# Side work of a two-layer diffusion step: the waits between its stages are set anew

## Chip, core and metric

One core of one Trainium2 chip runs the whole program in one launch. The metric is the device time of an execution in microseconds, as the median of several.

## What is computed

One inference step of a two-layer network over 384 columns: 128 context tokens and 256 latent tokens, model width 1024. Per layer (from the reference):

```python
h = _rmsnorm(x, norm_mix[d]) * (1.0 + ca) + sa        # sa, ca, ga, sm, cm, gm from silu(c) @ w_mod[d] + b_mod[d]
q, k, v, gb, gc, xin, u, vs = _project(h, w_in[d])
q = _apply_axial_rope(q, rope); k = _apply_axial_rope(k, rope)      # latent tokens only
att = _diff_attention(q, k_all, v_all, lam, subln[d], lam_init)     # softmax(1) - lam * softmax(2), then rmsnorm
conv = gb * _short_conv(gc * xin, conv_w[d], conv_b[d])
cmlp = _chunk_mlp(u, vs, w_s[d], b_s[d])
x = x + ga * (concat([att, conv, cmlp]) @ w_out[d])
h = _rmsnorm(x, norm_mlp[d]) * (1.0 + cm) + sm
x = x + gm * (relu(h @ w_up[d]) ** 2 @ w_down[d])
```

There are four attention heads, each with two 64-dim components of q and k; the context keys and values of the cache come in front of the latent ones. A final rmsnorm ends it; the new context keys and values are outputs too.

## The kernel before

**Products.** Activations lie transposed, features on the partitions, 384 columns wide. Each weight chunk of 128 x 1024 (512 KB, tile `raw`) is loaded by SyncE's DMA queue (L187), cut by ScalarE into a rounded high part (`whi`, L201) and by VectorE into the rest (`wlo`, L203). A product step, `mm3` at L217, is three matmuls: high weights by high activations, high by low, low by high (L220, L221, L222; L449 to L451 where tokens are the rows, `nat`). Activations are split the same way: `hh` and `hl`.

**Order of a layer.** Mixer: keys and queries of the first heads (`pkq`; three heads in layer 0, two in layer 1), values (`nat`, 512 wide), then `pk` and `pq` of the remaining heads and two short convolutions of three products each (`pgc`, `pxi`, `pgb`), then the chunk inputs (`nat`, 256 wide) and `pu`, then the output product `po2`. After it the MLP in two halves (`pup`, `pdn`). In layer 0 TensorE also does the products with `wmod` that give five of the modulation vectors (`pm`, L262, in groups of two loads), and VectorE does the others as long weighted sums (L315, tile `junk`), a pair for each load.

**Side work.** Everything else is side work: the norm and its scaling (`normed`, L370 hh on ScalarE, L373 hl on VectorE), rotary positions (`rope_apply`: a shuffle on VectorE, L656, then three steps on GpSimd, L657 to L659), the split of keys (`keys`: kh casts on ScalarE, L674 and L677, kl on VectorE, L678), of queries (`queries`: L690 and L693), attention, convolution, and the column sums of the shift (`shift_products`: `psh`, its copy `shb` at L468, `psb` at L472). An attention unit is one head by one block of 128 query columns; three units make a head. In it come the scores `sc` (L738 to L742), the negative row maximum `nm` (L746), the exponentials (L751), their scaling (L755 to L759), transposes `pt` (L763), the copy `ats` (L774); the last unit of a head then does `po`, probabilities by values (L786), squares (L792), the rsqrt and its refinement, the scaled `o` (L801), transposes `pot` (L807) and the result into `y` (L810, L812).

**What sets the order.** Nothing is scheduled at run time: TensorE, ScalarE, VectorE and GpSimd carry out their instructions in the order in which the program issues them, and each waits for its inputs. Side work is written as Python generators that yield between two stages. `yield n` says that the next stage is issued n ticks later, and `tick` is called after every product step, where it issues every stage that has come due:

```python
    def tick(n=1):
        for _ in range(n):
            clock[0] += 1
            while queue and queue[0][0] <= clock[0]:
                step()
```

The numbers n stand in the table `WAIT` (L35), one entry for each place, as a pair for layer 0 and layer 1. So a number there sets how many product steps TensorE does between one stage and the next, and with it the place of the stage in the queue of each engine. An instance, the end of an attention unit:

```python
            yield wt["at6"]
            cols = slice(h * P, h * P + P)
            po = acc_tile("po")
```

Here `at6` ticks lie between the issue of the copy `ats` and that of the products `po` that read it. Likewise `k0` lies ahead of the rotation of a key, `k1` between the rotation and the kh casts of L674, `k2` ahead of the casts of L677; `q0`, `q1`, `q2` do this for queries; `fh0` lies ahead of the third head of `first_heads`; `mods` is the number of ticks between two groups of `pm`, `sums0` the delay of the first L315. `mods0` and `sums0` are read in layer 0 only.

Of the kernel before, what the change touches and what calls it, by code (L numbers as in the profile page):

```python
# [31 lines left out]


WAIT = {
    "sums_up": (8, 7),  # L35
    "sums_down": (5, 0),
    "hid0": (1, 1),
    "hid1": (3, 3),
    "later": (4, 4),
    "later2": (4, 6),  # L40
    "spread": (2, 0),
    "final": (4, 3, 3, 3),
    "rstd": (3, 9),
    "at0": (1, 1),
    "at1": (2, 1),
    "at2": (3, 3),
    "at3": (2, 2),
    "at4": (5, 5),
    "at5": (1, 3),
    "at6": (4, 2),  # L50
    "at7": (2, 2),
    "at8": (2, 2),
    "at9": (2, 2),
    "at10": (3, 4),
    "at11": (1, 1),
    "at12": (1, 1),
    "k0": (1, 1),
    "k1": (5, 5),
    "k2": (1, 3),
    "q0": (1, 1),  # L60
    "q1": (5, 6),
    "q2": (1, 2),
    "fh0": (14, 14),
    "fh1": (2, 5),
    "fh2": (2, 2),
    "fh3": (5, 5),
    "cv0": (1, 3),
    "cv1": (2, 2),
    "cv2": (2, 3),
    "cm0": (1, 1),  # L70
    "sy": (2, 2),
    "normed": (3, 3),
    "wait_normed": (1, 12),
    "mix": (4, 4),
    "heads": (4, 1),
    "mods": (9, 0),
    "mods0": (2, 0),
    "sums": (7, 0),
    "sums0": (58, 0),
    "unit0": (24, 24),  # L80
    "head": (24, 24),
    "late": (0, 5),
# [1029 lines left out]
```

## Time and profile before

| | us |
|---|---|
| Median of three executions | 907.21 (906.78 to 910.43) |
| Profiled execution | 906.61 |
| Its span, first to last instruction | 904.8 |
| TensorE busy | 876.9 |
| VectorE busy | 651.6 |
| ScalarE busy | 481.7 |
| GpSimd busy | 84.2 |

The mean granted clock of TensorE is 0.995 of full speed. In the rows below a time is the start in microseconds from the start of the span, then follow the duration, the engine, the line, the operation, the tiles (out<-in), their shape and, in brackets, how long the engine was idle before it and what ended that. A row of waits reads: engine and line that waited, what it waited for, the total in microseconds, how many times, the longest.

### The profile page before, as it was taken

The page shows a single profiled execution, that of the slowest core. Times are in us where ns is not written, and L with a number is a line of the kernel's source. Part 1 is how long each engine was busy: PE and PEld are TensorE (multiplying, and loading weights), DVE is VectorE, ACT ScalarE, POOL GpSimd, SP SyncE. Part 2 cuts the span into 40 slices and gives each one's busy share as a digit, 9 for nine tenths or more (in the row PEclk, how much of TensorE's full clock was granted, in tenths as well). Part 3 has the DMA queues.
Part 4 walks back from the last instruction along what each step waited for, and adds up shares of the span by engine and source line. Part 5 has one row for each costly group of instructions (what it writes and reads, how often), then busy time and mean ns, then how long its engine had stood idle before and what let it go on. Part 6 is the DMA issues. An engine that isn't in the chain of part 4 may idle for free.

```text
span 904.8 us, 14504 instructions
## 1 busy us (share of the span) xinstructions
PE 876.9 (97%) x5476; PEld 841.8 (93%) x5476; DVE 651.6 (72%) x1214; ACT 481.7 (53%) x949; POOL 84.2 (9%) x84
## 2 busy tenths in 40 slices
PE   5999989999999999999998999999999999999996
PEld 4867878999999999999997889999999999999996
DVE  5697887889888777889979877568886334555333
ACT  4568765447662236654336786444675223665331
POOL 1013310030000000000113340002000000000021
PEclk9999999999999999999999999999999999999998
DMA  9977657555667655557663323234565333433302
GB/s 346 330 280 258 231 168 271 167 166 167 205 190 235 230 187 190 197 189 236 213 218 102 131 73 117 92 97 134 175 220 167 123 133 117 133 124 118 116 1 70
DMA packets 48470, 156.55 MB, mean 173 GB/s; under 512 B 5392, under 2 KB 11024, under 8 KB 48400
## 3 DMA queue, kind: packets, MB, share of 16 engines
q1 hardware_dynamic: 48400, 155.63, 51.8%
q8 instruction: 43, 0.70, 0.3%
q14 instruction: 27, 0.22, 0.1%
HBM read 152.98 MB, written 2.62 MB: 172 GB/s over the span
## 4 chain that ended last, share of the span: by engine, by line
PE 84%; DVE 7%; ACT 4%; POOL 2%; issue 1%; DMA 1%; SPq 0%; DVEq 0%; ACTq 0%; POOLq 0%
PE pdn L220 10%; PE pdn L222 10%; PE pdn L221 10%; PE pup L221 10%; PE pup L220 9%; PE pup L222 9%; PE po L220 2%; PE po L221 2%; PE po L222 2%; PE pm L262 2%; PE pkq L220 2%; PE pkq L221 2%; PE pkq L222 1%; DVE wlo L203 1%; POOL rt L658 1%
## 5 line engine op out<-in xcount | busy, mean ns | idle before, releaser
L201 ACT CAST whi<-raw 128x1024 fp32r<-128x1024 f32 x182 | 190.4, 1052 | 286.8 <-PE pdn L221 153.9
L203 DVE TENSOR_TENSOR wlo<-raw,whi 128x1024 fp32r<-128x1024 f32 x182 | 224.6, 1240 | 61.4 <-ACT whi L201 61.2
L220 PE MATMUL pdn<-ah,whi 128*128 128x384 f32 (+2 forms) x528 | 174.7, 331 | 0.0
L221 PE MATMUL pdn<-al,whi 128*128 128x384 f32 (+2 forms) x528 | 174.6, 331 | 0.0
L222 PE MATMUL pdn<-ah,wlo 128*128 128x384 f32 (+2 forms) x528 | 174.6, 331 | 0.0
L220 PE MATMUL pup<-hh,whi 128*128 128x386 f32 x512 | 174.2, 340 | 0.0
L221 PE MATMUL pup<-hl,whi 128*128 128x386 f32 x512 | 173.7, 339 | 0.3
L222 PE MATMUL pup<-hh,wlo 128*128 128x386 f32 x512 | 172.8, 338 | 0.0
L315 DVE SCALAR_TENSOR_TENSOR junk<-raw,cb 128x1024 bf16<-128x1024 f32 x112 | 136.7, 1220 | 0.4
L221 PEld LDWEIGHTS pdn<-al,whi 128*128 128x128 f32 x528 | 99.2, 188 | 0.0
L220 PEld LDWEIGHTS pdn<-ah,whi 128*128 128x128 f32 x528 | 99.2, 188 | 0.0
L222 PEld LDWEIGHTS pdn<-ah,wlo 128*128 128x128 f32 x528 | 99.2, 188 | 0.0
L221 PEld LDWEIGHTS pup<-hl,whi 128*128 128x128 f32 x512 | 96.9, 189 | 1.1 <-DVE hl L388 0.9
L220 PEld LDWEIGHTS pup<-hh,whi 128*128 128x128 f32 x512 | 96.4, 188 | 0.3
L222 PEld LDWEIGHTS pup<-hh,wlo 128*128 128x128 f32 x512 | 96.5, 188 | 0.0
L337 POOL TENSOR_TENSOR sacc<-sacc,sq 128x384 f32<-128x384 f32 x23 | 29.6, 1285 | 667.5 <-ACT sq L330 533.6
L927 ACT ACTIVATE relu<-relu,ub 128x128 f32<-128x128 f32 (+1 forms) x128 | 51.3, 449 | 17.4 <-DVE relu L924 17.4
L399 DVE SCALAR_TENSOR_TENSOR x<-pdn,modv,x 128x128 f32<-128x128 f32 (+1 forms) x62 | 23.0, 413 | 43.9 <-PE pdn L222 43.9
L931 DVE TENSOR_TENSOR al<-relu,ah 128x384 fp32r<-128x384 f32 x64 | 35.6, 556 | 15.2 <-ACT ah L929 14.9
L220 PE MATMUL po<-y,whi 128*128 128x384 f32 x128 | 43.0, 336 | 0.0
L222 PE MATMUL po<-y,wlo 128*128 128x384 f32 x128 | 42.8, 334 | 0.0
L221 PE MATMUL po<-y,whi 128*128 128x384 f32 x128 | 42.8, 334 | 0.0
(202 smaller groups left out, 1413.7 us busy)
## 6 DMA issues: line engine op xcount, KB each, us to landing
raw<-in_wall_dram SPq DMA_DIRECT2D x182, 512.0 KB, 3.6
raw<-in_wmodT_dram SPq DMA_DIRECT2D x56, 512.0 KB, 4.3
raw<-in_wmod_dram SPq DMA_DIRECT2D x40, 512.0 KB, 5.7
raws<-in_wall_dram SPq DMA_DIRECT2D x6, 512.0 KB, 7.1
x<-in_xT_dram SPq DMA_DIRECT2D x8, 192.0 KB, 8.0
out_dram<-x SPq DMA_DIRECT2D x4, 256.0 KB, 2.6
mix<-in_cv_dram SPq DMA_DIRECT2D x2, 256.0 KB, 5.0
mix<-in_ws_dram SPq DMA_DIRECT2D x2, 256.0 KB, 5.2
```

The source lines that it names most:

```text
L201: nc.scalar.copy(hi, r)
L203: nc.vector.tensor_sub(lo, r, hi.bitcast(F32))
L220: mm(out, wh[wsl], ah[asl], start=first, stop=False)
L221: mm(out, wh[wsl], al[asl], start=False, stop=False)
L222: mm(out, wl[wsl], ah[asl], start=False, stop=last)
L262: mm(pm[32 * j : 32 * j + 32, own], sct[:, kt, :], w[:, (4 * k + j) * width : (4 * k + j + 1) * width], start=(kt == 0), stop=(kt == KT - 1),)
L315: nc.vector.scalar_tensor_tensor(junk, w, 1.0, cb[:, g], ALU.mult, ALU.mult, accum_out=mr[:, dt, g : g + 1])
L337: eng.tensor_add(stat["acc"], stat["acc"], sq)
L399: nc.vector.scalar_tensor_tensor(x[:, dt, a:b], pacc[:, a:b], gate[:, dt, g : g + 1], x[:, dt, a:b], ALU.mult, ALU.add)
L658: nc.gpsimd.tensor_mul(s, s, rp[:, 1])
L927: nc.scalar.activation(r[:, s0:s1], r[:, s0:s1], AF.Relu, bias=ub[:, g : g + 1])
L931: nc.vector.tensor_sub(al[:, i], r, ah[:, i].bitcast(F32))
```

## The change

Only numbers of `WAIT` change. The same instructions are issued, and the sum of work of each engine is the same. The core of the diff, the entries of which the text speaks:

```diff
-    "at6": (4, 2),
+    "at6": (2, 2),
-    "k0": (1, 1),
-    "k1": (5, 5),
+    "k0": (1, 3),
+    "k1": (9, 6),
-    "q2": (1, 2),
-    "fh0": (14, 14),
+    "q2": (2, 4),
+    "fh0": (8, 14),
-    "mods": (9, 0),
+    "mods": (7, 0),
-    "sums0": (58, 0),
+    "sums0": (61, 1),
...
```

Changed as well: `sums_up` (8, 7) to (8, 8), `hid0` (1, 1) to (1, 3), `hid1` (3, 3) to (3, 4), `spread` (2, 0) to (1, 0), `rstd` (3, 9) to (3, 10), `at7` (2, 2) to (3, 3), `at8` (2, 2) to (2, 3), `at11` (1, 1) to (2, 1), `at12` (1, 1) to (2, 3), `cv0` (1, 3) to (1, 5), `sy` (2, 2) to (4, 1), `wait_normed` (1, 12) to (2, 12), `mods0` (2, 0) to (2, 1).

The order of instructions differs in the first two thirds of layer 0's mixer and the start of its `po2`, in layer 1's mixer, and on VectorE and ScalarE in the first half of layer 1's MLP. GpSimd's order is the same throughout.

ScalarE, layer 0, ahead of the copy shb that the shift product psb reads. kh are the key casts, qs the query casts, e the exponentials; - stands before, + now:

```order
-L201 CAST whi<-raw 128x1024
+L677 CAST kh<-mix 64x384 x2
+L201 CAST whi<-raw 128x1024
+L751 ACTIVATE e,s<-sc,nm 128x128 x2
 L674 CAST kh<-mix 64x384 x2
-L677 CAST kh<-mix 64x384 x2
-L751 ACTIVATE e,s<-sc,nm 128x128 x2
 L690 CAST qs<-mix 64x256 x2
 L757 ACTIVATE e<-e,s 128x128
 L468 COPY shb<-psh 128x256
+L677 CAST kh<-mix 64x384 x2
```

The second casts of one head have moved behind shb, and those of the head before it have moved up to this place from further ahead.

ScalarE, layer 0, at the products pk and pq of the fourth head. L725 and L726 copy the new queries, L774 is the copy ats:

```order
-L674 CAST kh<-mix 64x384 x2
-L757 ACTIVATE e<-e,s 128x384
-L774 COPY ats<-pt 128x3x128
-L677 CAST kh<-mix 64x384 x2
+L757 ACTIVATE e<-e,s 128x384
+L774 COPY ats<-pt 128x3x128
 L201 CAST whi<-raw 128x1024
 L725 ACTIVATE qp_106<-pq 64x128 x2
 L726 ACTIVATE mix<-pq 128x256
+L674 CAST kh<-mix 64x384 x2
 L751 ACTIVATE e,s<-sc,nm 128x128 x2
+L677 CAST kh<-mix 64x384 x2
```

Both pairs of kh casts, ahead of the query copies before, stand behind them now.

VectorE, layer 1, during the values product, before. t and hl are the norm's tiles, kl_104 the low part of a key, rt the rotation's:

```order
L656 STREAM_SHUFFLE rt<-mix 128x256
L678 TENSOR_TENSOR kl_104<-mix,kh 64x384 x2
L203 TENSOR_TENSOR wlo<-raw,whi 128x1024
L362 SCALAR_TENSOR_TENSOR t<-x,amix_94,rstd 128x128
L362 SCALAR_TENSOR_TENSOR t<-x,amix_94,rstd 128x256
L373 SCALAR_TENSOR_TENSOR hl<-t,modv_92,hh 128x128
L373 SCALAR_TENSOR_TENSOR hl<-t,modv_92,hh 128x256
```

The same place now:

```order
L656 STREAM_SHUFFLE rt<-mix 128x256
L203 TENSOR_TENSOR wlo<-raw,whi 128x1024
L362 SCALAR_TENSOR_TENSOR t<-x,amix_94,rstd 128x128
L362 SCALAR_TENSOR_TENSOR t<-x,amix_94,rstd 128x256
L373 SCALAR_TENSOR_TENSOR hl<-t,modv_92,hh 128x128
L373 SCALAR_TENSOR_TENSOR hl<-t,modv_92,hh 128x256
L678 TENSOR_TENSOR kl_104<-mix,kh 64x384 x2
```

The two subtractions kl_104 stand behind this pair of hl.

More of the change, by code (lines that the diff above doesn't have):

```diff
@@ L34 @@
 WAIT = {
-    "sums_up": (8, 7),
+    "sums_up": (8, 8),
     "sums_down": (5, 0),
-    "hid0": (1, 1),
-    "hid1": (3, 3),
+    "hid0": (1, 3),
+    "hid1": (3, 4),
     "later": (4, 4),
     "later2": (4, 6),
-    "spread": (2, 0),
+    "spread": (1, 0),
     "final": (4, 3, 3, 3),
-    "rstd": (3, 9),
+    "rstd": (3, 10),
     "at0": (1, 1),
@@ L49 @@
     "at5": (1, 3),
-    "at6": (4, 2),
-    "at7": (2, 2),
-    "at8": (2, 2),
+    "at6": (2, 2),
+    "at7": (3, 3),
+    "at8": (2, 3),
     "at9": (2, 2),
     "at10": (3, 4),
-    "at11": (1, 1),
-    "at12": (1, 1),
-    "k0": (1, 1),
-    "k1": (5, 5),
+    "at11": (2, 1),
+    "at12": (2, 3),
+    "k0": (1, 3),
+    "k1": (9, 6),
     "k2": (1, 3),
@@ L66 @@
     "fh3": (5, 5),
-    "cv0": (1, 3),
+    "cv0": (1, 5),
     "cv1": (2, 2),
@@ L70 @@
     "cm0": (1, 1),
-    "sy": (2, 2),
+    "sy": (4, 1),
     "normed": (3, 3),
-    "wait_normed": (1, 12),
+    "wait_normed": (2, 12),
     "mix": (4, 4),
     "heads": (4, 1),
-    "mods": (9, 0),
-    "mods0": (2, 0),
+    "mods": (7, 0),
+    "mods0": (2, 1),
     "sums": (7, 0),
-    "sums0": (58, 0),
+    "sums0": (61, 1),
     "unit0": (24, 24),
```

## The prediction

> **What bounds the kernel now.** I read the page first: busy times, the row of granted clock, the chain that ended last.
>
> ```profile
> PE 876.9 (97%) x5476; PEld 841.8 (93%) x5476; DVE 651.6 (72%) x1214; ACT 481.7 (53%) x949; POOL 84.2 (9%) x84
> PEclk9999999999999999999999999999999999999998
> PE 84%; DVE 7%; ACT 4%; POOL 2%; issue 1%; DMA 1%; SPq 0%; DVEq 0%; ACTq 0%; POOLq 0%
> ```
>
> TensorE is busy for 876.9 of 904.8 us at nearly full clock, so all its idle time is 904.8 - 876.9 = 27.9 us. The change takes no product away, so it can only move this idle time. Next I read what PE waited for.
>
> ```profile
> PE po L786 <- ACT ats L774: 3.4, 2, 2.6
> PE nat L451 <- DVE hl L373: 2.8, 1, 2.8
> PE sc L741 <- ACT e L751: 1.3, 2, 0.8
> PE psb L472 <- ACT shb L468: 1.1, 1, 1.1
> PE pt L763 <- DVE e L759: 0.6, 2, 0.4
> PE pm L262 <- DMA raw<-in_wmod_dram: 0.3, 1, 0.3
> PE pot L807 <- DVE o L801: 0.3, 1, 0.3
> ```
>
> These seven groups (total, times, longest) add up to 9.8 us. All are waits of a side product or of `nat` inside a mixer; no wait of that view lies between the mixers, in the long MLP products, apart from the start and the end, which the new spacing leaves alone. So 9.8 us is the most that can be won here, about 1.1%. The third view, PE's timeline around each, says where they are.
>
> ```profile
> 79.12 0.61 PE L472 MATMUL psb<-sel,shb 128*128 128x2 f32 x4 [1.13 <-ACT shb L468]
> ...
> 114.15 0.34 PE L221 MATMUL pgc<-hl,whi 128*128 128x384 f32 x1
> 114.33 0.34 PE L222 MATMUL pgc<-hh,wlo 128*128 128x384 f32 x1
> 114.88 0.52 PE L763 MATMUL pt<-ident,e 128*128 128x128 f32 x3 [0.22 <-DVE e L759]
> ...
> 122.24 0.94 PE L786 MATMUL po<-mix,ats 128*128 128x128 f32 x6 [2.60 <-ACT ats L774]
> ...
> 497.81 0.50 PE L451 MATMUL nat<-whi,hl 128*128 128x512 f32 x1 [2.79 <-DVE hl L373]
> ...
> 506.67 0.44 PE L741 MATMUL sc<-kh,qs 128*128 128x384 f32 x1 [0.43 <-ACT e L751]
> ...
> 523.13 0.44 PE L741 MATMUL sc<-kh,qs 128*128 128x384 f32 x1 [0.82 <-ACT e L751]
> ...
> 526.32 0.94 PE L786 MATMUL po<-mix,ats 128*128 128x128 f32 x6 [0.81 <-ACT ats L774]
> ```
>
> The four up to 122 us are layer 0, the rest layer 1. A stall costs a little more than its bracket. Matmuls of this form start 0.18 us apart (114.15, 114.33), yet the transposes start 0.55 after 114.33: 0.37 lost where the bracket says 0.22, so 0.15 more for each stall. A product step of three matmuls is 3 x 0.18, about 0.53 us.
>
> **The change part by part.** Every wait here follows from in-order queues: a stage issued early, whose input is late, holds what stands behind it. The working goes stall by stall.
>
> *Layer 0, the shift product at 79.12.* ACT's queue ahead of it, before:
>
> ```profile
> 73.71 1.05 ACT L674 CAST kh<-mix 64x384 fp32r<-64x384 f32 x2 [0.30 <-POOL mix L659]
> ...
> 76.91 0.84 ACT L690 CAST qs<-mix 64x256 fp32r<-64x256 f32 x2 [0.25 <-POOL mix L659]
> ...
> 78.72 0.35 ACT L468 COPY shb<-psh 128x256 f32<-128x256 f32 x1
> ```
>
> `k1` 5 to 9 takes one pair of kh casts (1.05) ahead of this place, and what it had waited for (0.30), behind the step of L706, so the rotation on POOL starts about 1.3 us sooner; the shb copy moves up with it and the 1.13 us go. Arithmetic says 1.35 against 1.13, a thin margin. I take -1.1. A second pair of kh casts stands behind shb now, where nothing of PE's waits.
>
> *The two small ones (114.88, the pot of 0.27, 0.5 together) and the DMA wait (0.3).* `fh0` 14 to 8 and `k1` clear DVE's and ACT's queues there; SP issues the wmod loads sooner, because the lambda load ahead of them is no longer held by a buffer that PE reads. Price: -0.5 and -0.3. Each load is consumed later than it lands, and the SP queue holds nothing else that PE needs soon.
>
> *The stall of 2.60 at 122.24.* ACT, and POOL's rotations on both sides of it:
>
> ```profile
> 111.25 1.05 ACT L674 CAST kh<-mix 64x384 fp32r<-64x384 f32 x2 [1.64 <-POOL mix L659]
> ...
> 113.34 1.04 ACT L677 CAST kh<-mix 64x384 fp32r<-64x384 f32 x2
> ...
> 115.92 0.39 ACT L726 ACTIVATE mix<-pq 128x256 f32<-128x256 f32 x1
> ...
> 121.72 0.46 ACT L774 COPY ats<-pt 128x384 f32<-128x384 f32 x1
> ```
> ```profile
> 108.78 1.62 POOL L658 TENSOR_TENSOR rt<-rt,rp 128x256 f32<-128x256 f32 x1 [0.79 <-DVE rt L656]
> ...
> 117.14 1.72 POOL L658 TENSOR_TENSOR rt<-rt,rp 128x256 f32<-128x256 f32 x1
> ```
>
> ACT sat 1.64 us at the kh casts, then spent 1.05 and 1.04 on them, all ahead of L726, whose output starts the rotation that ends in the late ats. In the changed order both pairs stand behind L726: 3.7 us less ahead of it. If the rotation keeps its length, ats starts at 118.0 and `po` could start at about 118.5. PE was there at 122.24 - 2.60 = 119.6; `at6` 4 to 2 brings it two steps (1.05) earlier, the stall that goes at 114.88 another 0.37, and one more wmod product group (`mods` 9 to 7, 1.07 us each, row below) ahead of it brings it back: 119.3. So ats has some 0.8 us to spare. I take -2.4; if half of the shift is lost behind other ACT and DVE work, it is -1.3; it cannot be better than -2.6.
>
> *A new wait in the next head.* The same `at6` moves the next `po`, of which the trace shows:
>
> ```profile
> 140.39 0.46 ACT L774 COPY ats<-pt 128x384 f32<-128x384 f32 x1
> ```
> ```profile
> 136.54 1.07 PE L262 MATMUL pm<-raw,sct 128*32 128x256 f32 x16
> ...
> 140.75 0.28 PE L449 MATMUL nat<-whi,hh 128*128 128x256 f32 x1
> ...
> 141.10 0.38 PE L786 MATMUL po<-mix,atp 128*128 128x128 f32 x2
> ```
>
> ats was done at 140.85, `po` came at 141.10: 0.25 us of slack. Two steps of cover (0.7 here, a narrower `nat` step goes from 140.75 to 141.10) and the wmod group at 136.54 go from ahead of it, 1.8 in all; the attention chain moves up with PE only as far as DVE lets it. Between 0 and +1.6; I take +0.5, nearer the low end, since the chain's own transposes move up by the 1.07 as well. The wmod groups themselves cost PE the same wherever they stand: 0.
>
> Four stalls gone and one new one make 3 x 0.15, -0.5. Layer 0: -0.3 - 1.1 - 0.5 - 2.4 + 0.5 - 0.5 = **-4.3** (bounds -5.2 and -1.9).
>
> *Layer 1, 497.81 and 506.67.* Here DVE is the bound, not a single late step:
>
> ```profile
> 493.14 1.55 DVE L678 TENSOR_TENSOR kl<-mix,kh 64x384 fp32r<-64x384 f32 x2
> ...
> 497.41 0.74 DVE L373 SCALAR_TENSOR_TENSOR hl<-t,modv,hh 128x128 fp32r<-128x128 f32 x2
> ```
> ```profile
> 493.32 0.95 POOL L658 TENSOR_TENSOR rt<-rt,rp 128x256 f32<-128x256 f32 x1 [4.50 <-DVE rt L656]
> 494.36 0.93 POOL L659 TENSOR_TENSOR mix<-rt 128x256 f32<-128x256 f32 x1
> ```
> ```profile
> 495.31 0.82 ACT L690 CAST qs<-mix 64x256 fp32r<-64x256 f32 x2 [1.86 <-POOL mix L659]
> 497.13 0.91 ACT L370 ACTIVATE hh<-t,modv 128x128 fp32r<-128x128 f32 x2 [0.99 <-DVE t L362]
> ```
>
> `k0` 1 to 3 puts the two kl subtractions (1.55 us) behind the hl that PE waits for. But hl needs hh, hh stands on ACT behind qs, and qs waits for POOL. The shuffle ahead of L658 is now followed by a wlo subtraction instead of kl, the pattern of 108.78, where L658 took 1.62, not 0.95. Then L659 ends at 493.32 + 1.62 + 0.08 + 0.93 = 495.95, qs at 496.8, and hl starts 0.28 after hh does, as before, at 497.1: 0.3 us earlier than 497.41. The 1.55 of kl still follow ahead of the row maximum that releases 506.67, so that wait grows by 1.55 - 0.3: **+1.2**. With L658 at its 0.95 the same working gives +0.5, and if POOL also gives DVE back what they took from each other, -0.5; with both POOL steps as long as the 1.72 at 117.14, +2.2. [...]
>
> *523.13 and 526.32.*
>
> ```profile
> 518.04 1.05 ACT L674 CAST kh<-mix 64x384 fp32r<-64x384 f32 x2 [0.40 <-POOL mix L659]
> ...
> 522.62 0.37 ACT L751 ACTIVATE e<-sc,nm 128x128 f32<-128x128 f32 x1
> ```
>
> The kh casts move behind L726 and their second half behind this exp: one pair less ahead of it, 1.05 us, so 0.82 goes. The `po` wait after it lives on the same queue and moves up by about as much as PE does, so its 0.81 stays: -1.0 for both, between 0 and -1.6. The remaining pt wait (0.4, the longer of its group) goes: with its restart -0.5, at worst 0. Layer 1: +1.2 - 1.0 - 0.5 = **-0.3**. Layer 1's other numbers (`hid0`, `hid1`, `sums_up`) move ACT and DVE work only where PE waits for neither: 0.
>
> **Sum.** -4.3 - 0.3 = -4.6. The profiled execution took 906.6 us (span 904.8 and 1.8 around it); the median of three is 907.2, 0.6 higher. So 902.0 by the profile and **902.6** beside the median, -0.51%.
>
> **The rivals.** A difference under 0.5% (4.5 us, a time above 902.7) is about what a measurement of this kernel cannot tell from no change.
>
> - *The DVE stretch loosens.* POOL and DVE stop colliding around 493 (-0.5 in place of +1.2) and both waits at 523 and 526 go (-1.6 in place of -1.0): -6.9, 900.3 us. For it: DVE has little else to lose there. Against: the shuffle now stands directly ahead of a wlo. Chance 0.25.
> - *POOL is held longer*, +2.2 in place of +1.2, and the waits at 523 and 526 stay: -2.6, 904.6 us. For it: 1.62 and 1.72. [...] Chance 0.16.
> - *The late ats only halves* (-1.3) and the new `po` wait is +1.6: -2.4, 904.8 us. Chance 0.11.
> - *Slower: `po` in front of its ats, head after head.* `at6` takes two steps of cover from every one of layer 0's groups of `po`, and PE held there also holds the pq product that the next head's rotation starts from, so a wait like 2.60 comes back each time. Four heads at 2.60 are +10.4, against -2.2 of other gains: +8.2, 915.4 us. It decides from the third such wait on (7.8 - 2.2 > 4.5). Against it: the slack of 0.8 above. Chance 0.08.
>
> The forecast itself has 0.40, and half of its spread (about 2 us to each side) lies beyond 902.7. Faster by over 0.5%: 0.25 + 0.21 = 0.46; within: 0.19 + 0.16 + 0.11 = 0.46; slower: 0.08. The range runs from a little under the first rival, 899.8, to 906.6, past the second and third with their terms against me together.
>
> **What would show it.** Right: among PE's waits no psb on shb, no wait for a wmod load; po on ats well under 1 us in layer 0; ACT's L726 near 111, with the kh casts after it. Around 497 the `nat` wait is hardly shorter than 2.79, or it is and the `sc` wait has grown by the same; POOL's L658 there reads about 1.6. Wrong: a po wait of over 1 us around 117 or 138; L658 at 0.75 to 0.95 with both layer 1 waits gone; any wait of PE in the MLP stages; or PE's busy time changed by more than 1 us, which would say that the clock moved and not the waits.

## The result and the profile after

| | before | after |
|---|---|---|
| Median of the executions set against each other (6 each) | 908.74 us | 903.34 us |
| All of them | 906.78 to 910.62 | 902.15 to 903.96 |
| Profiled execution, span | 906.61, 904.8 | 903.88, 902.1 |

The ratio is 0.9937, with a 95% interval of 0.9924 to 0.9949: 0.63% faster, 5.4 us at the medians. The forecast was 902.6 us and 0.51%.

What TensorE waited for in the profile after, the rows that answer to those of before (total, times, longest):

```profile
PE nat L451 <- DVE hl L373: 1.9, 1, 1.9
PE sc L741 <- ACT e L751: 1.7, 1, 1.7
PE po L786 <- ACT ats L774: 1.4, 2, 1.2
PE pm L262 <- DMA raw<-in_wmod_dram: 1.3, 1, 1.3
PE pt L763 <- DVE e L759: 1.1, 1, 1.1
PE psb L472 <- ACT shb L468: 0.5, 1, 0.5
```

The `pm` row is not the wait of before: it stands at 7.85 us, on one of the first loads, in code that is the same in both kernels. The other rows on PE's timeline:

```profile
79.44 0.61 PE L472 MATMUL psb<-sel,shb 128*128 128x2 f32 x4 [0.49 <-ACT shb L468]
...
120.83 0.49 PE L786 MATMUL po<-mix,ats 128*128 128x128 f32 x2 [0.20 <-ACT ats L774]
...
493.63 0.50 PE L451 MATMUL nat<-whi,hl 128*128 128x512 f32 x1 [1.92 <-DVE hl L373]
...
503.76 0.44 PE L741 MATMUL sc<-kh,qs 128*128 128x384 f32 x1 [1.69 <-ACT e L751]
...
522.61 0.49 PE L786 MATMUL po<-mix,ats 128*128 128x128 f32 x2 [1.22 <-ACT ats L774]
...
536.08 0.44 PE L763 MATMUL pt<-ident,e 128*128 128x128 f32 x2 [1.05 <-DVE e L759]
```

In layer 0, 1.13 became 0.49, 2.60 became 0.20, and the waits of 0.30, 0.22 and 0.27 are gone. In layer 1, the four places read 2.79, 0.43, 0.82 with 0.81, 0.39 before and 1.92, 1.69, 0 with 1.22, 1.05 now: 5.2 us of waiting before, 5.9 after. Read as a distance, so that the start drops out: from the fifth of the first shift products (54.33 before, 55.81 after) to the first short gap of TensorE in the MLP (203.35 and 200.16) it was 149.02 us and is 144.35, 4.7 less. From there to the same gap of layer 1 (628.95 and 625.89) it was 425.60 and is 425.73. So the traces say: **4.7 us, all of it in layer 0's mixer, and nothing in layer 1.** The span shows only 2.7 of it because this execution happened to wait 1.3 us for a load at the start, which the profiled one of before did not.

That leaves a question. The medians are 5.4 us apart (7.2 for one variant below), more than 4.7, and the executions of before scatter over 4 to 5 us where those of the changed kernel stay within 2.

ScalarE after, at the place where before it stood 1.64 us in front of the key casts, waiting for POOL:

```profile
111.47 0.61 ACT L757 ACTIVATE e<-e,s 128x384 f32<-128x384 f32 x1 [2.45 <-DVE s L756]
...
113.86 0.39 ACT L726 ACTIVATE mix<-pq 128x256 f32<-128x256 f32 x1
114.14 1.03 ACT L674 CAST kh<-mix 64x384 fp32r<-64x384 f32 x2
...
116.03 1.03 ACT L677 CAST kh<-mix 64x384 fp32r<-64x384 f32 x2
...
120.32 0.46 ACT L774 COPY ats<-pt 128x384 f32<-128x384 f32 x1
```

L726 now stands ahead of both pairs of casts, but ScalarE waits 2.45 us for VectorE ahead of it, so it starts only 2.1 us earlier than before (113.86 against 115.92). ats is there at 120.78, and `po` has to wait 0.2 for it.

### The profile page after: what moved, and what is told of

Same layout as the page of the kernel before. It is cut to its first block, busy times and chain, and to the rows that moved or that the text cites. A ratio compares the mean times of both kernels' runs of the same rounds, so it can differ in the third digit from the quotient of the medians.

```text
span 902.1 us, 14515 instructions
## 1 busy us (share of the span) xinstructions
PE 876.5 (97%) x5476; PEld 843.3 (93%) x5476; DVE 653.7 (72%) x1214; ACT 479.6 (53%) x949; POOL 83.5 (9%) x84
## 4 chain that ended last, share of the span: by engine, by line
PE 86%; DVE 6%; ACT 3%; issue 2%; DMA 1%; POOL 1%; SPq 0%; DVEq 0%; ACTq 0%; POOLq 0%
PE pdn L221 10%; PE pdn L222 10%; PE pdn L220 10%; PE pup L221 10%; PE pup L220 10%; PE pup L222 9%; PE po L222 2%; PE po L221 2%; PE po L220 2%; PE pm L262 2%; PE pkq L220 2%; PE pkq L221 2%; DVE wlo L203 2%; PE pkq L222 1%; PE po L786 1%
## 5 line engine op out<-in xcount | busy, mean ns | idle before, releaser
L220 PE MATMUL po<-y,whi 128*128 128x384 f32 x128 | 43.0, 336 | 0.0
L923 DVE COPY ub<-pup 128x2 f32<-128x2 f32 x64 | 10.2, 159 | 45.0 <-PE pup L222 44.4
```

What stands on the lines that cost most here:

```text
L220: mm(out, wh[wsl], ah[asl], start=first, stop=False)
L923: nc.vector.tensor_copy(ub, pt[:, T:TE])
```

## The experiments

Each kernel was timed in five rounds against before on the same chip; a ratio is to before, with its 95% interval. The kernels came in three groups on two chips, where the median of before was 909.88, 908.79 and 909.60 us; kernels of different groups are compared by their ratios.

**One layer at a time.** `layer0_only` takes the first number of each changed pair, `layer1_only` the second.

> Layer 0's numbers as changed, layer 1's as before. Theory A (nearly all of the gain is layer 0's mixer, where stalls of 0.3, 0.6, 0.4, 2.4 and 0.4 us go): from the shift product at 55 us to the first MLP product at 200 us the trace is 4.5 to 4.8 us shorter than before, and the time is 4.5 to 5.5 us under before. Rival B (both layers bring a like part): 2 to 3 us.

> Layer 1's numbers as changed, layer 0's as before. Theory A: within 0.5 us of before; PE waits about 1.9 us at nat, 1.7 at sc, 1.2 at po and 1.0 at pt in place of 2.8, 0.4 and 0.8, 0.8 and 0.4. Rival B: 2 to 3 us faster, the nat wait under 1.5 with no longer wait behind it.

Measured: 902.71 us, ratio 0.9929 (0.9917 to 0.9942), and 909.73 us, 1.0004 (0.9992 to 1.0017). Layer 0's numbers are the whole gain; layer 1's give nothing, as Theory A had it. The gain of `layer0_only` at the medians, 7.2 us from 909.88, is larger than its trace's (56.05 to 200.40 us, 144.35, again 4.7 less) and than Theory A said. `layer1_only` shows why. Its layer 0 is the code of before, yet its profile needs 151.5 us for the same distance (56.36 to 207.90), 2.5 more. The stretches of 80 to 90 and 120 to 130 us (start and end, length, then busy time of PE, PEld, DVE, ACT, POOL, then the granted clock, the DMA share and GB/s), first of before, then of `layer1_only`:

```profile
80.00:90.00 10.00, 10.00 (x70) 9.10 (x69) 6.51 (x16) 7.76 (x20) 0.73 (x1) 1.00 0.65 221
120.00:130.00 10.00, 7.50 (x48) 6.92 (x49) 8.10 (x22) 7.43 (x22) 0.53 (x1) 1.00 0.43 143
```
```profile
80.00:90.00 10.00, 8.93 (x44) 8.89 (x45) 7.23 (x18) 7.58 (x18) 0.00 (x0) 0.83 0.65 238
120.00:130.00 10.00, 7.43 (x39) 7.10 (x38) 8.72 (x19) 5.30 (x21) 3.88 (x3) 0.83 0.46 140
```

The clock column falls from 1.00 to 0.83, about 1 us behind the end of the psb wait (1.56 us there) and of the po wait (2.57). On PE's timeline of `layer1_only`:

```profile
82.14 0.51 PE L220 MATMUL pgc<-hh,whi 128*128 128x384 f32 x1
82.45 0.53 PE L221 MATMUL pgc<-hl,whi 128*128 128x384 f32 x1
...
85.33 0.44 PE L221 MATMUL pgc<-hl,whi 128*128 128x384 f32 x1
85.62 0.34 PE L222 MATMUL pgc<-hh,wlo 128*128 128x384 f32 x1
```

From 82.14 to 85.33 ten matmuls start 0.32 us apart instead of 0.18: 1.4 us lost a second time, after the wait was over. The profiled execution of before had the same two waits and no such dip. So a wait can cost more than its own length, here 1.56 us and 1.4 behind it, and only in some executions.

**Is it the idle time?** The next two kernels leave every wait of before in place and give PE useless work to do in it, products of the identity written to columns that nothing reads. The first try, `fill_idle`:

```diff
+        if t0:
+            for _ in range(8):
+                mm(po[:, P : 2 * P], ident, ident, start=True, stop=True)
...
+                if (d, h, i) == (0, 1, 2):
+                    for _ in range(16):
+                        mm(po[:, 3 * P : 4 * P], ident, ident, start=True, stop=True)
```

> Before, with useless products of the identity by itself (8 ahead of psb of the third head, 16 ahead of the late half of the po group), written to columns of the same PSUM tiles that nothing reads. They fill PE's idle time there and take no wait away. Theory F (a long idle of PE costs a second time, since at some of them the granted clock falls for some microseconds: matmuls 0.32 us apart in place of 0.18 between 82.1 and 85.3 of one run, about 1.5 us): granted clock 1.00 all through layer 0 in the profile, and the median 1 to 2.5 us under before, with few executions above 909.5. Rival G (the scatter of before comes from the first loads and the waits are all that counts): within 0.3 us of before, or slower by up to 0.5 where the filling overshoots.

Measured: 910.43 us, ratio 1.0019 (1.0009 to 1.0029). It overshot twice. One such product takes 0.22 us, so the 16 took 3.57 against a wait of 2.6; and the 8 stood in a tile that itself waited for shb, behind the wait of 1.53 instead of in it. But the clock was 1.00 all through layer 0, and 12 executions lay within 1.3 us (909.72 to 911.02). The time, slower where Theory F had 1 to 2.5 us faster, decides nothing between F and G, since the filling overshot. The second try, `fill_fit`, puts 5 into the last sc tile and 10 into po:

> Before, with fewer useless identity products than in the first try, put where they wait for nothing: 5 ahead of psb of the third head, into the free columns of the last sc tile, 10 ahead of the late half of the po group (0.22 us each by the first try, so 1.1 and 2.2 us, a little less than the waits). Theory F (long idles of PE cost a second time through the granted clock): no stretch of layer 0 under 1.00 in the profile, the times within 2 us of each other, median 1 to 2 us under before. Rival G (only the waits count): median within 0.4 us of before and the same scatter of 4 to 5 us.

Measured: 907.54 us, ratio 0.9982 (0.9970 to 0.9994), within 906.57 to 908.46, beside 906.31 to 911.48 for before: more instructions on the engine that bounds the kernel, and 2.1 us less at the medians (909.60 for before). Its stretches:

```profile
80.00:90.00 10.00, 10.00 (x69) 9.15 (x68) 6.75 (x16) 7.98 (x20) 0.58 (x1) 1.00 0.67 235
120.00:130.00 10.00, 9.34 (x63) 8.81 (x61) 7.98 (x23) 7.15 (x22) 0.73 (x1) 1.00 0.45 152
```

Theory F stands and Rival G falls: with layer 0's idle times cut to 0.4 us the dips and the scatter go. The mean clocks say the same: 0.994 to 0.997 in the 12 executions of `fill_fit`, 0.990 to 0.997 in those of before beside it, where those with 0.997 took 906.3 to 907.1 us and those with 0.990 took 909.5 to 911.5. The length of the wait alone does not say which ones cost twice: one of 1.56 us was followed by a fall of the clock in `layer1_only`, and the one of 2.60 in the profiled execution of before was not.

The record of the clock in the traces sets the two apart. Every dip in the mixers of the 14 kept traces is 3.41 us long (once two in a row), and each begins a whole number of 3.41 us after the clock's first 1.00 on record: 19, 32 and 142 of them in `layer1_only`, counted from 17.29 us. So in these traces the dips lie in a row of such stretches, which stands elsewhere against the program from trace to trace (142 to the dip at 499.36 in before, counted from 14.67 us; 140 to the one at 494.74 in after, from 16.88), and how long TensorE is idle within one stretch sorts them better than the length of a wait. All 15 full-clock stretches with 1.86 us of idle or more were followed by a dip (in before 495.95 to 499.36, with 1.86, in after 491.33 to 494.74, with 1.92); of the 12 between 1.56 and 1.82 two were (those at 1.56 and 1.75), and below 1.56 none was. Two stretches around the po wait of before, then two of `layer1_only` (columns as above):

```profile
117.07:120.48 3.41, 2.57 (x18) 2.38 (x16) 2.85 (x5) 0.00 (x0) 3.33 (x3) 1.00 0.29 85
120.48:123.90 3.42, 1.66 (x12) 1.67 (x13) 2.84 (x6) 3.29 (x8) 0.05 (x1) 1.00 0.68 220
```
```profile
123.10:126.52 3.42, 0.85 (x7) 0.85 (x8) 2.32 (x7) 2.48 (x6) 0.86 (x1) 1.00 0.81 267
126.52:129.93 3.41, 3.41 (x13) 3.32 (x13) 3.34 (x9) 2.33 (x12) 0.00 (x0) 0.50 0.34 89
```

The 2.60 us of before were cut in two, 0.84 and 1.76, and no dip followed; the 2.57 of `layer1_only` fell into one stretch. What sets the stretches no run shows.

**Which numbers of layer 0.** `k1_layer0` changes k1 alone, `mods_only` mods and sums0 (mods0 has the same number for layer 0 in both kernels).

> Only k1 of layer 0, 5 to 9. Theory C (the key casts on ScalarE ahead of the query copies make the long po wait): po on ats falls from 2.6 to under 1 us, psb on shb from 1.1 to about 0.5; 2 to 3 us faster. Rival D (what frees the chain is fewer stages on VectorE there, from fh0 and the others): po keeps over 2 us, under 1 us faster.

> Only mods 9 to 7, mods0 and sums0. Theory C: the wmod product groups only change places; the 0.3 us wait for a load may go, the po wait changes by what PE gets to do ahead of it, one group of 1.07 us: 2.6 to 1.5; 0 to 1.5 us faster. Rival E (the wmod groups as cover are the main thing): 2.5 us faster or more. Against both, slower by up to 1 us if the extra sums on VectorE come at a bad place.

Measured: 907.42 us, ratio 0.9974 (0.9963 to 0.9985), and 908.60 us, 0.9989 (0.9977 to 1.0002). k1 alone takes the long po wait away whole (2.6 to 0), so Theory C is right on that and Rival D wrong. But psb, which Theory C had at about 0.5, rises to 1.7, and a new wait appears. PE's waits with k1 alone:

```profile
PE psb L472 <- ACT shb L468: 1.7, 1, 1.7
PE pot L807 <- DVE o L801: 1.4, 1, 1.4
```

`mods_only` loses at a load and at psb (1.7) what it wins at po (1.9 left of 2.6); the extra cover is not the main thing, against Rival E. Why psb got worse is on POOL, first with k1 alone, then with k1 and wait_normed:

```profile
70.11 1.62 POOL L658 TENSOR_TENSOR rt<-rt,rp 128x256 f32<-128x256 f32 x1 [1.39 <-DVE rt L656]
```
```profile
68.72 0.74 POOL L658 TENSOR_TENSOR rt<-rt,rp 128x256 f32<-128x256 f32 x1 [0.73 <-DVE rt L656]
```

That led to `k1_normed` (k1 and wait_normed, 1 to 2) and `k1_normed_fh0` (and fh0, 14 to 8):

> Layer 0: k1 5 to 9 and wait_normed 1 to 2, nothing else. Theory H (with k1 alone POOL's L658 took 1.62 us beside a wlo at 69.9, and shb was late by 1.75; the later norm puts hl between shuffle and wlo again): L658 there 0.75, psb on shb falls to 0.4 to 0.8; pot on o stays at about 1.4; 1 to 1.5 us faster than with k1 alone. Rival I (shb is late for what stands on ScalarE): psb stays at 1.5 or more, same time as k1 alone.

> Layer 0: k1 5 to 9, wait_normed 1 to 2 and fh0 14 to 8. Theory N (fh0 puts the third head's stages earlier, off VectorE around 125, so that o is in time): pot on o falls from 1.4 to under 0.3, and the time comes to that of all of layer 0's numbers, 1.5 to 2 us under k1 and wait_normed alone. Rival O (the places of the wmod groups, mods, do it): pot stays at 1 us or more.

Measured: 904.80 us, ratio 0.9953 (0.9937 to 0.9968), and 902.89 us, 0.9937 (0.9920 to 0.9955). Their rows for psb and pot, the pair of two numbers first:

```profile
PE pot L807 <- DVE o L801: 1.4, 1, 1.4
...
PE psb L472 <- ACT shb L468: 0.5, 1, 0.5
```
```profile
PE psb L472 <- ACT shb L468: 0.5, 1, 0.5
PE pot L807 <- DVE o L801: 0.5, 1, 0.5
```

Theory H holds: the norm, a tick later, puts the short hl between the shuffle and wlo, POOL's step runs in 0.74, and shb comes 1.2 us earlier. Rival I would have left psb alone. Theory N holds for most of the pot wait (0.5, where under 0.3 had been expected). **Three numbers, k1, wait_normed and fh0 of layer 0, give the whole gain**; 902.89 is not told apart from 903.34 or 902.71.

**The moved po.** `layer0_old_po` is `layer0_only` with at6, at7, at11 and at12 as before (at8 is the same in layer 0 anyway).

> Layer 0's numbers as changed, but at6, at7, at8, at11 and at12 as before; layer 1 as before. Theory J (these five only keep the pot products from waiting once the po wait is gone): po on ats 0, pot on o 0.3 to 1.5, 0.3 to 1.5 us slower than with all of layer 0's numbers. Rival K (the shorter at6 costs what the prediction put at 0.5 us): 0.2 to 0.5 us faster than with all of them.

Measured: 902.98 us, ratio 0.9936 (0.9922 to 0.9950): the same as with them. Its po wait is 0 instead of 0.2, and no pot wait comes back. Theory J falls (something else, fh0 by the run above, keeps pot in time), and of Rival K's half microsecond nothing can be seen: no effect of these four numbers on the time shows.

**Layer 1.** Three kernels with all of layer 0's numbers: `layer0_and_k0` and `layer0_and_k1` with one number of layer 1 besides, and `all_but_k1`, the changed kernel with k1 of layer 1 back at 5.

> All of layer 0's numbers as changed, and of layer 1's only k0, 1 to 3. Theory P (VectorE bounds that stretch, so the wait only changes its place): nat on hl falls from 2.8 to 1.9, sc on e rises from 0.4 to 1.7, within 0.6 us of layer 0's numbers alone, the po and pt waits behind as without it (0.8 and 0.4). Rival Q (the step as predicted, 1.2 us lost): 1 us slower or more.

> All of layer 0's numbers as changed, and of layer 1's only k1, 5 to 6. Theory L (in layer 1 the later key casts free the exp at 523 and the rest of layer 1's numbers take it back): sc on e at 520 falls from 0.8 to under 0.2, po and pt stay at 0.8 and 0.4, 0.7 to 1 us faster than layer 0's numbers alone. Rival M (po and pt wait longer by what the exp is earlier, since VectorE's kl steps stand in the way): same time as layer 0's numbers alone, po 1.2 and pt 1.0.

> The changed kernel with k1 of layer 1 at 5 as before. Theory R (in layer 1 it is the later key casts that bring kl on VectorE in front of the reciprocals, so po and pt wait longer; the other numbers free the exp): po 0.8 or less in place of 1.2, pt 0.4 or less in place of 1.0, sc at 520 none; 0.5 to 1.2 us under the changed kernel and the fastest of all. Rival S (without the later casts the exp is late again): sc 0.8, same time as the changed kernel.

Measured: 906.09, 907.60 and 907.44 us, ratios 0.9969 (0.9956 to 0.9982), 0.9986 (0.9975 to 0.9996) and 0.9985 (0.9972 to 0.9997), where layer 0's numbers alone have 0.9929. None of the theories or rivals had this: each number by itself costs 3 to 5 us, and taking k1 out of the set costs 4. (Rival Q had 1 us or more for k0, but by a shorter nat and a longer sc wait, and neither came; Rival M had longer po and pt waits, but at the same time.) PE's waits with k0 alone, with k1 alone, and with all but k1:

```profile
PE po L786 <- ACT ats L774: 3.0, 2, 2.8
PE nat L451 <- DVE hl L373: 2.9, 1, 2.9
PE pt L763 <- DVE e L759: 1.7, 1, 1.7
```
```profile
PE nat L451 <- DVE hl L373: 2.8, 1, 2.8
PE po L786 <- ACT ats L774: 2.3, 2, 2.1
PE pt L763 <- DVE e L759: 1.9, 1, 1.9
```
```profile
PE po L786 <- ACT ats L774: 3.1, 2, 2.8
PE nat L451 <- DVE hl L373: 2.9, 1, 2.9
PE pt L763 <- DVE e L759: 1.7, 1, 1.7
```

Two things are shown. The nat wait stays at 2.8 to 2.9 with either number: neither alone moves kl behind hl, and without k1 the rest of the set does not either (that k0 is the partner it needs was not tested by itself). And po and pt wait far longer. With k1 alone the cause is on VectorE, where the kl step now runs ahead of the reciprocal that ats hangs on:

```profile
517.52 1.82 DVE L678 TENSOR_TENSOR kl<-mix,kh 64x384 fp32r<-64x384 f32 x2
519.37 1.65 DVE L203 TENSOR_TENSOR wlo<-raw,whi 128x1024 fp32r<-128x1024 f32 x1
520.95 0.15 DVE L755 RECIPROCAL s<-s 128x2 f32<-128x2 f32 x1
```

With k0 alone it is the same, and all but k1 has these rows 0.4 us later:

```profile
520.21 2.09 DVE L678 TENSOR_TENSOR kl<-mix,kh 64x384 fp32r<-64x384 f32 x2
522.33 0.17 DVE L755 RECIPROCAL s<-s 128x2 f32<-128x2 f32 x1
```

With layer 0's numbers alone kl stood at 515.64, took 1.14 us, and was long done when the reciprocal came at 520.50. With k1 alone and with all but k1 the clock also fell to 0.50 for one stretch behind the long po wait (from 523.54 and 526.01); what that cost there was not measured apart. A version that beats both kernels clearly did not come out of this; layer 0's numbers alone are as good as all.

## Why the prediction was right, and where not

- **PE's waits in the mixers are all there is to win: right for the traces.** The MLP of both layers is unchanged to 0.1 us.
- **The po wait, -2.4: right in size.** 2.60 to 0.20; `k1_layer0` shows that it is the key casts on ScalarE, as worked out. But L726 moved up by 2.1 us and not by 3.7, since ScalarE now waits 2.45 us for VectorE at L757; so the sign "L726 near 111" failed, and of the 0.8 us to spare nothing was left. The two rotation steps beside DVE's long ones kept their 1.7 and 1.6 us, as assumed.
- **psb, -1.1: half.** It fell by 0.64. Its cause was also only half seen: not the casts alone, which in `k1_layer0` made it worse, but POOL's step beside a wlo, and wait_normed, which the prediction does not mention.
- **The small waits and the load, -0.8: right.** All three are gone.
- **The new po wait, +0.5: did not come.** By `layer0_old_po` the at numbers change nothing that can be seen. The restarts, put at -0.5, come out near -0.8 if all that is left is theirs (4.67 less 3.83 of listed idle time, 0.30 + 0.64 + 0.49 + 2.40).
- **497.81 and 506.67, +1.2: the mechanism right, the size not.** The nat wait fell by 0.87 and the sc wait rose by 1.26, together +0.4. L658 there takes 1.62, as taken over from 108.78; but L659 took 0.72 rather than 0.93, so the dearer case, both steps as long as 1.72, did not come, and kl, moved to where POOL is idle, took 1.11 instead of 1.55. The step put it down to k0; k0 alone does not do it, and k1 is needed.
- **523 and 526, -1.0, and pt at 539, -0.5: wrong.** The first pair fell by 0.4, and pt rose by 0.66. The step counted what the later key casts do on ScalarE and forgot that the same stage issues kl on VectorE:

```profile
518.31 2.10 DVE L678 TENSOR_TENSOR kl<-mix,kh 64x384 fp32r<-64x384 f32 x2
520.44 0.17 DVE L755 RECIPROCAL s<-s 128x2 f32<-128x2 f32 x1
...
532.11 2.11 DVE L678 TENSOR_TENSOR kl<-mix,kh 64x384 fp32r<-64x384 f32 x2
534.25 0.17 DVE L755 RECIPROCAL s<-s 128x2 f32<-128x2 f32 x1
```

  These are rows of after. kl, 2.1 us beside POOL, now stands in front of each reciprocal, and ats and e come after it.
- **The sum** of -4.6 stands against 4.67 - 0.13 = 4.54 us in the traces. Layer 0 was worth 0.4 more than said and layer 1 0.4 less. That the sum fits this closely is partly luck: in layer 0 the new po wait that did not come makes up for the half of psb, and what layer 0 has over makes up for layer 1.
- **The step from the profile to the median: wrong.** It took the profiled execution of before as 0.6 us from the median. It was one of the quickest: no wait for a load at the start, no dip of the clock in layer 0. In 52 of the 81 executions of before beside the experiments the mean clock is 0.990 to 0.993, below the 0.995 of the profiled one, and the waits cost a second time; that is why the medians lie further apart than the traces. The time of 902.6 came within 0.8 us of 903.34, but both its ends were off: the median of before was 908.74 and not 907.2, and the gain 5.4 us and not 4.6. The prediction read the clock only as a mean.

In layer 1 the same dip costs nothing, which fits that VectorE bounds that stretch (busy for 7.14 of 7.31 us from 499.36 to 506.67 in before). Before had it from 499.36, behind the nat wait that ended at 497.81, and reached the sc at 506.67, 8.86 us later, with 0.43 of waiting. `fill_fit` had no dip there:

```profile
498.06 0.50 PE L455 MATMUL nat<-whi,hl 128*128 128x512 f32 x1 [2.83 <-DVE hl L377]
```
```profile
506.92 0.44 PE L748 MATMUL sc<-kh,qs 128*128 128x384 f32 x1 [1.89 <-ACT e L758]
```

Again 8.86 us, with 1.89 of waiting: what the clock does not take, the wait does.

## What to carry to other kernels

When a stage is moved, list every instruction that it issues, on each engine, and what each one now stands in front of: a cast on ScalarE that goes out of the way can bring its partner on VectorE into it. Numbers that space side work do not add up; one of them alone can cost 3 to 5 us in a set that is worth nothing, so a set is tried whole and then by leaving one out. And a wait of the bounding engine is worth more than its length where the clock falls behind it, as for 1.4 us behind one of 1.56 in `layer1_only`: compare executions, not one profile.

## What the runs showed of the hardware

- TensorE's granted clock fell to 0.50 after some idle times of 1.56 to 2.9 us inside a kernel that keeps it 97% busy: 3.41 us a time, matmuls 0.32 us apart instead of 0.18, 1.4 us lost where TensorE bounds the kernel (`layer1_only`, 82.14 to 85.33).
- The dips in the mixers of the 14 traces lay in a row of 3.41 us stretches. With 1.86 us of idle or more in one stretch the next was at 0.50 in 15 of 15, with 1.56 to 1.82 in 2 of 12, with less in none; in before a wait of 2.60 us, cut by the end of a stretch into 0.84 and 1.76, left the clock at 1.00.
- Useless products in the idle time made the kernel faster: 0.9982 (0.9970 to 0.9994), `fill_fit`.
- The same POOL step of 128 x 256 took 0.74 us (`k1_normed`, hl on VectorE behind the shuffle) or 1.62 us (`k1_layer0`, wlo there). The wait of psb that hangs on it was 0.5 and 1.7 us.
